# Delta rule's output projection as seven Strassen products over even and odd heads, with its weight sums made in DRAM and the gate sums moved into the attention

## The chip, the cores and the metric

The kernel runs on one core of one Trainium2 chip. The core has five engines that run side by side, each with an in-order queue of its own: PE (TensorE, matrix products), DVE (VectorE), ACT (ScalarE), POOL (GpSimd) and SP (SyncE, which mostly starts DMAs). They wait for each other by semaphores. The metric is the time of one execution on the device in microseconds (us), lower is better.

## The reference

One decoder layer on 512 tokens of 2048 channels, in float32. Two branches run from the same normalised input, and their gated sum goes through an output projection:

```python
mod = jax.nn.silu(c) @ w_ada + b_ada
shift, scale, gate = jnp.split(mod[:, None, :], 3, axis=-1)
h = rms_norm(x, norm_w) * (1.0 + scale) + shift
proj = h @ w_in
...
a_out = swa_attention(aq, ak, av, sinks).astype(x.dtype) * jax.nn.silu(ag)
y_a = a_out @ w_o_swa
...
o = gated_delta_rule(dq, dk, dv, g, beta)
o = rms_norm(o, dn_norm_w) * jax.nn.silu(dz.reshape(B, T, DN_V_HEADS, DN_HEAD_V).astype(f32))
y_b = o.reshape(B, T, DN_VAL).astype(x.dtype) @ w_o_dn

y = jax.nn.sigmoid(mg_a) * y_a + jax.nn.sigmoid(mg_b) * y_b
return x + gate * (y @ w_out)
```

The change concerns `o @ w_o_dn`, from 32 heads of 128 (4096 channels) to 2048, and where the sums for `gate` and the sums of the blocks of `w_out` are made.

## The kernel before

**Products.** Every large product is one stream of channel tiles on PE. `channel_tile` (line 244) takes 128 output channels for all 512 tokens: 16 steps over the contracted channels, and in each step `mm3` (line 237) issues three matmuls, high part by high part, high by low and low by high. The parts come from `split` (line 50): ACT casts a float32 tile to the type that PE takes (`hi`, line 52), DVE subtracts that from the tile (`lo`, line 53). The weights (128x128) are stationary, the tokens (512) move.

**Weights.** `plan` writes down the list of weight jobs in the order of use, 1 MB each for the projections. `load_job` (line 200) loads a job into one of two buffers `raw`; `split_half` splits half a job (128x1024) into one of three pairs `whi`, `wlo`; `half_done` marks the next split and, when both halves of a job are split, the next load.

**Order.** Behind every second step of a channel tile `pump()` is called, 8 times for a tile. It advances side jobs, which are generators: `go` starts one after so many pumps, `beside(gen, rate)` advances one at `rate` steps a pump. What the pump emits at that point stands there in the engines' queues. `drain` finishes such a job.

**Stages.** `startup`; `deltanet`, the heads in 16 pairs (scan, normalisation, gate z), with POOL working on the decay masks; `branch_b` (line 1023), which is rewritten; `attention` (line 1104); `finish`.

- In the heads' stage each pair ends with 8 transposes on PE (line 274, tile `pto`) and stores its two heads to `o_d`. Beside it `weight_sums`, at 0.13 steps a pump from the third pair on, copies x to the output and makes the sums of blocks of `w_out` in DRAM (tiles `wsm`): a copy of 1 MB from SP (line 684), and an accumulating DMA from POOL's queue (line 688) on top. `finish` has a Strassen step over `w_out` already and uses them.
- `branch_b` goes through the 4096 channels in two halves of 16 heads. For a half it loads `o_d` (16 pieces of 256 KB, `oraw`), splits it into `oh`, `ol`, computes two merge gates (channel tiles of another projection, into `ma_d`) and 16 channel tiles `od`. The first half's results go to `yb_d`; the second half's add them and multiply with (1 + `bth`), the other merge gate from `mb_d` (lines 1050 and 1051). Beside it, at 0.2, `gate` (line 1499) loads the 16 MB of its weights in pieces of 1 MB (`gw`, line 1505), multiplies each by one column of silu(c) and sums (DVE, line 1511), and closes with four matmuls by ones (`pgate`).
- `attention` computes keys, then four groups; a group is eight heads. `attend` (line 1230) works through four blocks of 128 tokens in a group, one chain each: scores `S` on PE (line 1249), mask and maximum on DVE (lines 1255, 1260), exponentials on ACT (line 1273, `sm`), the denominator `den` (line 1277) and the scaling of the eight heads on DVE (line 1281), transposes on PE (line 274, `pP`), products with the values (`O`, line 1300). In the queues the chains stand among the channel tiles of the group's projections.

## Time and profile before

| | |
|---|---|
| Time, median of 3 runs | 2922.81 us (2918.60 to 2924.77) |
| The profiled execution | 2922.19 us, of which the span is 2919.7 us |
| Granted TensorE clock, mean | 0.996 |
| PE busy | 98% of the span |
| DVE, ACT, POOL busy | 60%, 37%, 8% |
| Read from HBM, written | 429.42 MB, 97.20 MB |
| The heads' stage | up to about 1628 us |
| Output projection with its merge gates | 1628 to about 2030 us |
| Attention | 2057 to 2565 us |

The profile is one execution. A row of a group gives the line in the kernel, the engine, the operation and its tiles (output <- inputs), the shape, the count, then busy time, the mean length of one in ns, and how long the engine idled just before such instructions, with what ended most of it. A row of the timeline gives start, length, engine, line, tiles, and in brackets the idle time ahead of it and who ended it. A row of windows gives the stretch, its length, then the busy time of PE, PE's weight loads (PEld), DVE, ACT and POOL with the count of instructions, the granted clock, the share in which the DMA engines were busy, and GB/s.

### The profile page before, as it was taken

How to read it: one execution, taken by the hardware profiler on the slowest of the kernel's cores; microseconds unless marked ns; L12 is line 12 of the kernel's file. 1: busy time of each engine (PE TensorE's matmuls, PEld its weight loads, DVE VectorE, ACT ScalarE, POOL GpSimd, SP SyncE). 2: the span in 40 equal slices, each digit the busy share in tenths (PEclk: the TensorE clock that was granted, in tenths of full speed). 3: DMA queues.
4: the chain of work that ended last, by engine and by line, in shares of the span. 5: the costliest groups of instructions: out<-in, count | busy, mean ns of one | idle time of the engine just before them, and what ended most of it. 6: DMA issues, size and time to landing. Idle time of an engine off the chain costs nothing.

```text
span 2919.7 us, 37991 instructions
## 1 busy us (share of the span) xinstructions
PE 2868.2 (98%) x14556; PEld 2349.8 (80%) x14556; DVE 1740.0 (60%) x2853; ACT 1082.6 (37%) x2097; POOL 243.5 (8%) x234
## 2 busy tenths in 40 slices
PE   8899999999999999999999999999999999999999
PEld 6677888888888888888888788888788788788777
DVE  6775998777776554544444453434755655554565
ACT  4354333433334333333333322312334434432343
POOL 0022211101101111110000000000100000000010
PEclk9999999999999999999999999999999999999999
DMA  9747555635547664663332675554322223365575
GB/s 382 288 147 214 160 179 151 201 120 200 169 150 215 186 194 145 196 173 122 109 124 87 234 259 181 198 162 162 107 88 90 77 89 105 114 234 180 174 243 152
DMA packets 176615, 493.58 MB, mean 169 GB/s; under 512 B 72721, under 2 KB 75281, under 8 KB 134321
## 3 DMA queue, kind: packets, MB, share of 16 engines
q1 hardware_dynamic: 170834, 466.52, 47.3%
q0 software_dynamic: 5600, 24.64, 4.3%
q8 instruction: 114, 1.87, 0.3%
q14 instruction: 67, 0.55, 0.1%
HBM read 429.42 MB, written 97.20 MB: 180 GB/s over the span
## 4 chain that ended last, share of the span: by engine, by line
PE 87%; DVE 5%; issue 4%; ACT 2%; DMA 2%; POOL 1%; SPq 0%; DVEq 0%; POOLq 0%; ACTq 0%
PE mm L240 24%; PE mm L242 23%; PE mm L241 23%; PE m L241 1%; PE m L242 1%; PE m L240 1%; DVE wa L414 1%; PE S L1249 1%; PE pv L959 1%; PE po L978 1%; PE O L1300 1%; PE pP L274 1%; DVE wlo L53 1%; PE pd L974 1%; PE po L977 1%
## 5 line engine op out<-in xcount | busy, mean ns | idle before, releaser
L240 PE MATMUL mm<-hh,whi 128*128 128x512 f32 x2784 | 1132.0, 407 | 2.3 <-ACT whi L52 1.6
L242 PE MATMUL mm<-hh,wlo 128*128 128x512 f32 x2784 | 1090.6, 392 | 1.1 <-DVE wlo L53 1.1
L241 PE MATMUL mm<-hl,whi 128*128 128x512 f32 x2784 | 1088.1, 391 | 0.0
L53 DVE TENSOR_TENSOR wlo<-raw,whi 128x1024 fp32r<-128x1024 f32 (+1 forms) x428 | 527.3, 1235 | 497.5 <-ACT whi L52 492.8
L52 ACT CAST whi<-raw 128x1024 fp32r<-128x1024 f32 (+1 forms) x428 | 445.5, 1043 | 933.3 <-PE mm L241 905.5
L242 PEld LDWEIGHTS mm<-hh,wlo 128*128 128x128 f32 x2784 | 523.0, 188 | 115.3 <-DVE wlo L53 1.9
L240 PEld LDWEIGHTS mm<-hh,whi 128*128 128x128 f32 x2784 | 524.3, 188 | 112.7 <-issue 8.4
L241 PEld LDWEIGHTS mm<-hl,whi 128*128 128x128 f32 x2784 | 524.8, 189 | 99.2 <-issue 0.8
L240 PE MATMUL mm<-oh,whi 128*128 128x512 f32 x512 | 200.3, 393 | 1.1 <-ACT whi L52 0.9
L241 PE MATMUL mm<-ol,whi 128*128 128x512 f32 x512 | 199.4, 390 | 1.0 <-DVE ol L53 1.0
L242 PE MATMUL mm<-oh,wlo 128*128 128x512 f32 x512 | 199.4, 390 | 0.5 <-DVE wlo L53 0.5
L755 POOL TENSOR_TENSOR E<-E,neg_g 128x512 f32<-128x512 f32 x64 | 81.3, 1270 | 482.2 <-DMA E<-g_rows 331.3
L805 DVE TENSOR_TENSOR A<-A,atmp 128x62 f32<-128x62 f32 (+30 forms) x124 | 114.3, 922 | 1.5
L240 PEld LDWEIGHTS mm<-oh,whi 128*128 128x128 f32 x512 | 96.1, 188 | 22.8 <-ACT whi L52 1.3
L241 PEld LDWEIGHTS mm<-ol,whi 128*128 128x128 f32 x512 | 96.1, 188 | 22.6 <-DVE ol L53 2.0
L242 PEld LDWEIGHTS mm<-oh,wlo 128*128 128x128 f32 x512 | 96.1, 188 | 21.0 <-DVE wlo L53 1.3
L798 DVE TENSOR_TENSOR atmp<-A 128x62 f32<-128x62 f32 (+30 forms) x124 | 109.9, 886 | 1.5
L906 POOL TENSOR_TENSOR qe<-qe,yq 128x512 f32<-128x512 f32 x32 | 48.6, 1537 | 725.3 <-DMA qe<-eg_rows 617.6
L53 DVE TENSOR_TENSOR wlo<-raww,whi 128x1024 fp32r<-128x1024 f32 x56 | 68.2, 1221 | 41.3 <-ACT whi L52 41.3
L52 ACT CAST whi<-raww 128x1024 fp32r<-128x1024 f32 x56 | 59.0, 1053 | 75.5 <-PE m L242 66.3
L952 DVE SCALAR_TENSOR_TENSOR r<-pp,neg_eg,vt 128x128 f32<-128x128 f32 x96 | 29.2, 346 | 78.8 <-PE pp L949 77.6
L1273 ACT ACTIVATE sm<-sm,mx,rs 128x256 f32<-128x256 f32 (+1 forms) x128 | 71.7, 562 | 3.3 <-DVE mx L1268 3.3
(328 smaller groups left out, 3126.5 us busy)
## 6 DMA issues: line engine op xcount, KB each, us to landing
raw<-in_w_ch SPq DMA_DIRECT2D x158, 1024.0 KB
wa<-in_w_ada_ss SPq DMA_DIRECT2D x32, 1024.0 KB
raw<-in_w_od SPq DMA_DIRECT2D x32, 1024.0 KB
E<-g_rows SPq DMA_DIRECT2D x64, 256.0 KB
wsm<-in_w_out POOLq DMA_DIRECT2D x16, 1024.0 KB, 9.9
gw<-in_w_ada_gate SPq DMA_DIRECT2D x16, 1024.0 KB
raw<-in_w_os SPq DMA_DIRECT2D x16, 1024.0 KB
raww<-wsm SPq DMA_DIRECT2D x16, 1024.0 KB
```

Source lines behind the costliest of these rows:

```text
L52: self.nc.scalar.copy(out=hi, in_=src)
L53: self.nc.vector.tensor_tensor(out=lo, in0=src, in1=hi.bitcast(F32), op=ALU.subtract)
L240: nc.tensor.matmul(ps, lhsT=wh, rhs=xh, start=first, stop=False)
L241: nc.tensor.matmul(ps, lhsT=wh, rhs=xl, start=False, stop=False)
L242: self.last_mm = nc.tensor.matmul(ps, lhsT=wl, rhs=xh, start=False, stop=last).ins
L274: self.nc.tensor.transpose(dst[:, c * P : (c + 1) * P], src_cols(c), self.ident)
L755: nc.gpsimd.tensor_tensor(out=E, in0=E, in1=ng, op=ALU.add)
L798: eng.tensor_tensor(out=t, in0=A[:, m : m + 1, m + 1 :].to_broadcast([P, m, n]), in1=A[:, :m, m : m + 1].to_broadcast([P, m, n]), op=ALU.mult,
L805: eng.tensor_tensor(out=A[:, :m, m + 1 :], in0=A[:, :m, m + 1 :], in1=t, op=ALU.add)
L906: nc.gpsimd.tensor_tensor(out=qf, in0=qf, in1=q, op=ALU.mult)
L952: nc.vector.scalar_tensor_tensor(out=r[:, e, :], in0=pp[:, e, :], scalar=self.neg_eg[:, c, 2 * g + e : 2 * g + e + 1], in1=v[e][:, c, :], ...
L1273: nc.scalar.activation(t, t, AF.Exp, scale=r[:, h : h + 1], bias=mx[:, h : h + 1], accum_out=den[:, h : h + 1])
```

## The change

The 4096 x 2048 product is written as a 2x2 block product: the contracted channels are split into even and odd heads, the tokens into the first and last 256, the output channels into two blocks of 1024. It is computed with seven products of sums (a form of Strassen's) instead of eight.

- `head_sums`: when a pair of heads is done, its four operand sums are made (four DVE operations of 128x256, in the tile `osb`), and seven operands are stored to `oq_d` with three DMAs, in place of two for `o_d`.
- `od_sums`: four sums of weight blocks, 8 tiles of 1 MB each, are made in DRAM (`od_d`) beside the heads from the third pair on, at 0.08 steps a pump: 32 copies from SP and 32 accumulating DMAs from POOL. `weight_sums`, for `w_out`, moves to the attention at 0.17, with its copies of x.
- `branch_b`: seven products of 16 steps. In a step the activations (128 channels by 128 tokens) are stationary and the weights (512 of 1024 columns) move, for two blocks of columns and two of tokens, three matmuls each, and one pump. The operands come in pieces of 256 KB, split six ahead. Weight jobs: 56 of 1 MB in place of 32. Results are tokens by channels; `evict` combines them in `k1`, `k5` and `c` (ACT copies for m1 and m5, DVE for the rest), and `od_store` turns them with eight transposes on PE, multiplies with (1 + merge gate) and stores to `yb_d`. Two merge gates run before the products and two behind them. The PSUM pools become six buffers for results and two for transposes.
- `gate` moves to the attention at 0.48, in four passes of 512 columns: 64 loads of 256 KB into one buffer and 64 multiplications of 128x512, with the closing matmul at the end of each pass.

```diff
@@ plan
-        for half in range(2):
-            ma(range(5 + 2 * half, 7 + 2 * half))
-            jobs += [(f"od{half}_{j}", a["w_od"][half, j]) for j in range(KT)]
+        ma(range(5, 7))
+        for m, (name, _, w) in enumerate(self.od_order()):
+            src = a["w_od"][w] if w else self.od_d[name]
+            jobs += [(f"od{m}_{b}", src[b]) for b in range(8)]
+        ma(range(7, 9))
@@ deltanet
-                        self.beside(self.ordered(self.weight_sums()), 0.13, "ws")
+                        self.beside(self.ordered(self.od_sums()), 0.08, "ws")
...
+    def od_order(self):
+        return [
+            ("m1", 0, (0, 0)), ("m2", 1, (1, 0)), ("m5", 3, None), ("m6", 4, None), ("m7", 5, None), ("m4", 2, None),
+            ("m3", 6, (1, 1)),
+        ]
+
+    def od_sums(self):
...
+        steps = [
+            [("m7", w[0, 1]), ("m5", w[0, 0])], [("m7", w[1, 1]), ("m5", w[0, 1])],
+            [("m6", d["m7"])], [("m6", w[0, 0])], [("m4", d["m6"])], [("m4", w[1, 0])],
+        ]
+        for slot in range(20):
+            todo = [(n, src, b) for b in range(8) if 0 <= slot - 2 * b < 6 for n, src in steps[slot - 2 * b]]
+            for i, (n, src, b) in enumerate(todo):
+                if slot % 2:
+                    nc.gpsimd.dma_start(out=d[n][b], in_=src[b], accum_op=ALU.add, max_dma_last_dim=8192)
+                else:
+                    nc.sync.dma_start(out=d[n][b], in_=src[b], max_dma_last_dim=8192)
+                if i % 2:
+                    yield
+            if len(todo) < 3:
+                yield
...
+    def head_sums(self, g, z, s):
...
+        TT(out=s[:, 0], in0=z[0][:, hi], in1=z[1][:, hi], op=ALU.subtract)
+        STT(out=s[:, 1], in0=s[:, 0], scalar=-1.0, in1=z[0][:, lo], op0=ALU.mult, op1=ALU.subtract)
+        TT(out=s[:, 2], in0=z[0][:, lo], in1=z[0][:, hi], op=ALU.add)
+        STT(out=s[:, 3], in0=s[:, 1], scalar=-1.0, in1=z[1][:, lo], op0=ALU.mult, op1=ALU.subtract)
+        for q, src in ((slice(0, 1), z[0][:, lo].unsqueeze(1)), (slice(1, 3), z[1].rearrange("p (q t) -> p q t", q=2)), (slice(3, 7), s)):
+            nc.sync.dma_start(out=self.oq_d[q, g // 2].rearrange("q p k t -> p q k t")[:, :, g % 2, :], in_=src)
@@ branch_b
+            for m, (name, _, _) in enumerate(order):
+                ps = {}
                 for kt in range(KT):
...
+                    u = 8 * m + kt // 2
+                    if kt % 2 == 0:
+                        split(u + 6)
+                    oh, ol = parts[u]
+                    hi, lo = self.half(f"od{m}_{kt // 2}")
+                    for n in range(2):
+                        w = slice(n * T, n * T + T)
+                        for t in range(2):
+                            if kt == 0:
+                                ps[n, t] = self.pmm.tile([P, T], F32, tag="mm", name="od")
+                            x = (oh[:, kt % 2, t * P : t * P + P], ol[:, kt % 2, t * P : t * P + P])
+                            self.mm3(ps[n, t], x, (hi[:, w], lo[:, w]), kt == 0, kt == KT - 1)
+                            if kt == KT - 1:
+                                evict(name, n, t, ps[n, t])
+                        self.pump()
+                    self.half_done()
...
+    def od_store(self, wk, half, j, c):
...
+        for q in range(2):
+            pt = self.ptp.tile([P, 2, 256], F32, tag="tp", name="pty")
+            for i in range(2):
+                for t in range(2):
+                    s = slice((2 * q + i) * P, (2 * q + i) * P + P)
+                    nc.tensor.transpose(pt[:, i, t * P : t * P + P], c[t][:, s], self.ident)
+            yield 1
+            y = wk.tile([P, 2, 256], F32, tag="yb", name="yb", bufs=3)
+            nc.vector.scalar_tensor_tensor(out=y, in0=mb[q], scalar=1.0, in1=pt, op0=ALU.add, op1=ALU.mult)
+            yield 1
...
@@ attention
+            self.beside(self.ordered(self.weight_sums()), 0.17, "ws")
+            self.beside(self.gate(keep), 0.48, "gate")
@@ gate
-        for kt in range(KT):
-            w = wk.tile([P, D], F32, tag="gw", name="gw", bufs=1)
-            nc.sync.dma_start(out=w, in_=a["w_ada_gate"][kt])
...
+            acc = wk.tile([P, T], F32, tag="vch0", name="gate_bc")
+            for kt in range(KT):
+                w = wk.tile([P, T], F32, tag="vch1", name="gw")
+                nc.sync.dma_start(out=w, in_=a["w_ada_gate"][kt][:, sl])
+                yield
...
+                    nc.vector.scalar_tensor_tensor(out=acc, in0=w, scalar=s, in1=acc, op0=ALU.mult, op1=ALU.add)
+                yield
```

Two places show how the queues are moved. DVE in the attention, first chain of the third group, from the sum that finishes the maxima to the denominator (`wlo` is a weight split, `ao` the end of the chain before). Before:

```order
L1263 TENSOR_TENSOR mx<-mx,rs 128x8
L1264 TENSOR_TENSOR mx<-mx,sink 128x8
L1266 TENSOR_TENSOR es<-sink,mx 128x8
L1268 TENSOR_SCALAR mx<-mx 128x8
L53 TENSOR_TENSOR wlo<-raw,whi 128x1024
L1307 TENSOR_TENSOR ao<-O,sg 128x4x128
L1277 TENSOR_TENSOR den<-den,es 128x8
```

After:

```order
L1372 TENSOR_TENSOR mx<-mx,rs 128x8
L1373 TENSOR_TENSOR mx<-mx,sink 128x8
L1375 TENSOR_TENSOR es<-sink,mx 128x8
L1377 TENSOR_SCALAR mx<-mx 128x8
L1624 SCALAR_TENSOR_TENSOR gate_bc<-gw,silu_c,gate_bc 128x512
L53 TENSOR_TENSOR wlo<-raw,whi 128x1024
L1416 TENSOR_TENSOR ao<-O,sg 128x4x128
L1624 SCALAR_TENSOR_TENSOR gate_bc<-gw,silu_c,gate_bc 128x512
L1386 TENSOR_TENSOR den<-den,es 128x8
```

Two steps of the gate stand between the negated maximum and the denominator, where there were none. The second place is DVE at the end of the fifth product (m7) of the new stage, which has no counterpart before (`od` is a result in PSUM, `k` and `c` the tiles that it is combined into, `ol` the split of an operand):

```order
L53 TENSOR_TENSOR ol<-oraw,oh 128x512
L53 TENSOR_TENSOR wlo<-raw,whi 128x1024
L1097 TENSOR_TENSOR k_13984<-od,k_13984 128x512
L1098 TENSOR_TENSOR c<-od,k_13985 128x512
L1097 TENSOR_TENSOR k_13984<-od,k_13984 128x512
L1098 TENSOR_TENSOR c<-od,k_13985 128x512
L1097 TENSOR_TENSOR k_13984<-od,k_13984 128x512
L1098 TENSOR_TENSOR c<-od,k_13985 128x512
L1097 TENSOR_TENSOR k_13984<-od,k_13984 128x512
L1098 TENSOR_TENSOR c<-od,k_13985 128x512
L53 TENSOR_TENSOR wlo<-raw,whi 128x1024 x2
```

Eight evictions stand between one weight split and the next.

133 lines of the change are left out of this document (84 added, 49 removed).

## The prediction

> **What bounds the kernel now.** I read the engine totals first, then the chain of waits by engine, then the groups of instructions.
>
> ```profile
> PE 2868.2 (98%) x14556; PEld 2349.8 (80%) x14556; DVE 1740.0 (60%) x2853; ACT 1082.6 (37%) x2097; POOL 243.5 (8%) x234
> PE 87%; DVE 5%; issue 4%; ACT 2%; DMA 2%; POOL 1%; SPq 0%; DVEq 0%; POOLq 0%; ACTq 0%
> L240 PE MATMUL mm<-oh,whi 128*128 128x512 f32 x512 | 200.3, 393 | 1.1 <-ACT whi L52 0.9
> ```
>
> PE is busy for 98% of the span, and 87% of the chain that ended last lies on it. The third row is one of the three product kinds of the stage that the change rewrites: 512 matmuls, waiting 1.1 us in all. Whatever shortens PE's stream there shortens the kernel, as long as no other engine stops the stream. Windows cut at the stages (us; busy of PE, PEld, DVE, ACT, POOL; granted clock; DMA share; GB/s) show how much room there is:
>
> ```profile
> 600.00:700.00 100.00, 99.10 (x531) 82.34 (x530) 74.09 (x120) 38.42 (x88) 15.72 (x12) 1.00 0.47 156
> 700.00:800.00 100.00, 99.06 (x520) 82.05 (x519) 74.63 (x115) 36.18 (x79) 9.71 (x9) 1.00 0.59 178
> 1400.00:1500.00 100.00, 100.00 (x523) 83.56 (x523) 49.98 (x100) 36.95 (x90) 12.10 (x11) 1.00 0.39 122
> 1628.00:1660.00 32.00, 30.89 (x137) 24.69 (x137) 18.41 (x21) 12.19 (x17) 0.00 (x0) 1.00 0.79 268
> 1660.00:2030.00 370.00, 368.57 (x1616) 302.61 (x1615) 152.50 (x140) 92.12 (x107) 1.00 (x2) 1.00 0.59 201
> 2057.00:2565.00 508.00, 508.00 (x2856) 408.12 (x2856) 300.50 (x595) 205.11 (x445) 25.56 (x18) 1.00 0.29 97
> 2785.00:2850.00 65.00, 64.19 (x284) 52.71 (x283) 44.01 (x50) 28.27 (x30) 6.93 (x8) 1.00 0.82 247
> ```
>
> The heads run to about 1628, the output projection of the delta rule to 2030, the attention from 2057 to 2565. In every one PE idles by less than 1% or so, and the attention, which receives two moved side jobs, has no PE idle at all. So the gain is a count of matmuls, and the question is what the moved work does to the others.
>
> **The matmuls.** The change issues 1344 products for 1536: 192 fewer, of the same shape (128 stationary columns, 512 moving), whichever operand is stationary. Their spacing is read from two rows of the old stage, 75 matmuls apart (25 of each of the three kinds):
>
> ```profile
> 2009.64 0.39 PE L240 MATMUL mm<-oh,whi 128*128 128x512 f32 x1
> 2026.64 0.39 PE L240 MATMUL mm<-oh,whi 128*128 128x512 f32 x1
> ```
>
> 17.00 / 75 = 226.7 ns each (0.39 is one matmul's length, which overlaps the next). 192 x 226.7 ns = **-43.5 us**.
>
> **The transposes.** Results come out as tokens by channels, and 64 transposes of 128x128 turn them. The heads' own transposes give the price:
>
> ```profile
> 1627.84 1.26 PE L274 MATMUL pto<-ident,osb 128*128 128x128 f32 x8 [0.17 <-DVE osb L1009]
> 1628.85 0.49 PE L242 MATMUL mm<-hh,wlo 128*128 128x512 f32 x1
> ```
>
> Eight take PE from 1627.84 to 1628.85, 1.01 us, 0.126 us each: 64 are **+8.1 us**. Here the Trainium skill speaks against the change: its page "TensorE: Matmul & The Clock Gate", section "Part 4: PE-mode transpose", puts one transpose in a kernel's context at some 275 ns. By that figure the 64 would be an estimated 17.6 us and the time 2916; this case's rows disagree with it, at 0.126 for eight in a row, so it gets no chance of its own.
>
> **Waits that go.** The old stage begins by loading 16 pieces of o beside the 1 MB gate weights; the first of its two windows idles 1.1 us, the second 1.4. The new one prefetches four operands behind two merge gates and has no gate weights beside it: **-2.5 us** (bounds 0 and -2.5).
>
> **Sums of heads.** Four DVE operations of 128x256 for each of 16 pairs, by these rows of the finishing stage:
>
> ```profile
> L1370 DVE TENSOR_TENSOR ya<-ya,yc 128x256 f32<-128x256 f32 x6 | 2.5, 422 | 11.5 <-DMA yc<-y_d 11.5
> L1371 DVE SCALAR_TENSOR_TENSOR ya<-ya 128x256 f32<-128x256 f32 x6 | 2.5, 419 | 0.1
> ```
>
> 64 x 0.42 = 27 us of DVE over a stage in which DVE is busy 50 to 75 us of each 100 and PE 99 to 100: **0** (with the cover gone, 27). Three DMAs for a pair in place of two go on SP behind the same generator; nothing of that stage reads them.
>
> **Weight sums in the heads' stage.** There were 16 copies on SP and 16 accumulating DMAs on POOL from the third pair on; now there are 32 and 32, at 0.08 steps a pump for 0.13. PE's idle in the two windows from 600 to 800, where the first old ones fall, is 0.90 + 0.94 us; later windows have none. Twice that would be +1.8 and none at all is possible: I take **+1** (0 to +4, the upper end twice the doubled value, since POOL waits in order for each copy).
>
> **Evictions in the new stage.** 28 results, eight DVE operations together behind each of products four and five (m6, m7), and per store four multiplies.
>
> ```profile
> L1051 DVE SCALAR_TENSOR_TENSOR yb<-bth,yb x16: 691/692/693, 1861.4 to 2028.2; 128x512 f32<-128x512 f32 x16
> L53 DVE TENSOR_TENSOR wlo<-raww,whi 128x1024 fp32r<-128x1024 f32 x56 | 68.2, 1221 | 41.3 <-ACT whi L52 41.3
> ```
>
> Eight at 0.69 hold DVE 5.5 us, and one weight split (1.22) is queued behind them. A half of weights now lasts 12 matmuls, 2.72 us; three halves are kept, so PE has about 5.4 us of split weights when the block begins, against 5.5 + 1.2. That is a shortage of 1.3 us at two products, and less at the others, whose store multiplies (0.69 each) fall among splits. I take **+5** (0 to 12, twice the whole block and a multiply).
>
> **Raw weights.** A 1 MB load used to serve 48 matmuls, 10.9 us; it now serves 24, 5.44 us, with the same two buffers. A buffer's round is 10.88 us, of which the split of its two halves takes about 2.7 + 0.8, so a load has some 7.4 us. The gate weights of the same size, issued and used here, bracket it:
>
> ```profile
> 1723.66 0.33 SPq L1505 DMA_DIRECT2D gw<-in_w_ada_gate  x1
> 1730.97 2.35 DVE L1511 SCALAR_TENSOR_TENSOR gate_bc<-gw,silu_c,gate_bc 128x2048 f32<-128x2048 f32 x1 [4.16 <-DMA gw<-in_w_ada_gate]
> 1740.99 0.33 SPq L1505 DMA_DIRECT2D gw<-in_w_ada_gate  x1
> 1745.85 2.35 DVE L1511 SCALAR_TENSOR_TENSOR gate_bc<-gw,silu_c,gate_bc 128x2048 f32<-128x2048 f32 x1 [2.62 <-DMA gw<-in_w_ada_gate]
> ```
>
> 4.86 us alone, 7.31 with a load of raw weights beside it. The new stage moves 1 MB and a 256 KB operand each 5.44 us, 241 GB/s, less than the 247 and 268 of two windows above. Just below the threshold: **0** (bounds 0 and, at 8.5 us a load, 28 rounds x 1.1 = 31).
>
> **Gate sums and out's weight sums in the attention.** The four matmuls that finish the gate only move: 0. What costs is DVE's queue. Sixteen chains (scores, mask, maximum, exponentials on ACT, denominator, eight scalings, then transposes on PE) run one behind another, and PE reaches the transposes shortly after DVE has finished. The first chain of the first group, then the second, third and fourth of a group and the first of the next:
>
> ```profile
> 2123.21 0.17 DVE L1277 TENSOR_TENSOR den<-den,es 128x8 f32<-128x8 f32 x1 [4.00 <-ACT sm L1273]
> 2123.65 1.66 DVE L1281 TENSOR_SCALAR sm<-sm,den 128x128 f32<-128x128 f32 x8
> 2127.41 1.03 PE L274 MATMUL pP<-ident,sm 128*128 128x128 f32 x8
> ...
> 2277.69 0.17 DVE L1277 TENSOR_TENSOR den<-den,es 128x8 f32<-128x8 f32 x1 [4.86 <-ACT sm L1273]
> 2278.13 2.19 DVE L1281 TENSOR_SCALAR sm<-sm,den 128x256 f32<-128x256 f32 x8
> 2281.82 1.04 PE L274 MATMUL pP<-ident,sm 128*128 128x128 f32 x8
> ...
> 2305.29 0.17 DVE L1277 TENSOR_TENSOR den<-den,es 128x8 f32<-128x8 f32 x1 [4.86 <-ACT sm L1273]
> 2305.73 2.19 DVE L1281 TENSOR_SCALAR sm<-sm,den 128x256 f32<-128x256 f32 x8
> 2308.49 1.03 PE L274 MATMUL pP<-ident,sm 128*128 128x128 f32 x8
> ...
> 2333.19 0.17 DVE L1277 TENSOR_TENSOR den<-den,es 128x8 f32<-128x8 f32 x1 [1.70 <-ACT sm L1273]
> 2333.63 2.19 DVE L1281 TENSOR_SCALAR sm<-sm,den 128x256 f32<-128x256 f32 x8
> 2338.32 1.03 PE L274 MATMUL pP<-ident,sm 128*128 128x128 f32 x8
> ...
> 2350.59 0.17 DVE L1277 TENSOR_TENSOR den<-den,es 128x8 f32<-128x8 f32 x1 [2.11 <-ACT sm L1273]
> 2351.46 0.30 PE L274 MATMUL pP<-ident,sm 128*128 128x128 f32 x1
> ```
>
> From the end of the scalings to PE's transposes there are 2.10, 1.50, 0.57, 2.50 and no us (in the last the transposes follow the scalings one by one). In brackets is what DVE waits for ACT before the denominator: 4.00, 4.86, 4.86, 1.70, 2.11. By the order of DVE after the change, gate steps stand before the negated maximum in chains one to four of the groups 3, 2, 1, 2; 0, 0, 2, 2; 0, 0, 2, 1; 0, 1, 0, 0 times, and in the wait for ACT 2, 1, 0, 1; 1, 0, 1, 1; 2, 0, 1, 1; 2, 0, 0, 0 times. A step is 0.69 us and the wait w for its weights, whose single buffer is refilled only behind the step before; queued behind a step that waits are the chain's own operations and the weight splits that PE needs. The plan issues a load 1 / 0.48 = 2.08 pumps of six matmuls, 2.83 us, ahead of its use. Loads of this size:
>
> ```profile
> 1655.03 2.65 DMA oraw<-o_d
> 746.89 5.69 DMA qe<-eg_rows
> ```
>
> 2.65 with little beside it, 5.69 beside the copies of x to the output, which now move here too: w lies between 0 and 2.86. A chain is late by its steps before the maximum, plus what its other steps exceed ACT's wait by, less the margin. Summed over the sixteen: w = 0 gives 1.7 us, 1.0 gives 16, 2.0 gives 40, 2.86 gives 63. The 36 moved copies of 1 MB, at 4.86 to 7.31 us each, run for 175 to 263 of 508 us, so w averages 1.0 to 1.5; the attention's DMA share is only 0.29, half that of the window of the slow load, so I take 1.0: **+16 us** (2 to 63). The Trainium skill, "DMA: Bandwidth & Descriptors", section "Issuing engines are not separate DMA queues", says that transfers started by any engine share the 16 DMA engines and interleave. The two rows agree as far as they go; it gives no price, and by it moving the sums to POOL's queue would not spare the gate's loads.
>
> **The sum.** -43.5 + 8.1 - 2.5 + 0 + 1 + 5 + 0 + 16 = -15.9, against the profiled execution: its span is 2919.7 us, with 2.5 around it 2922.19, 0.6 below the median 2922.81. 2922.19 - 15.9 = 2906.3: **2906 us**.
>
> **Rivals.** *All hidden* (0.13): evictions fit between splits and gate loads arrive in time, -43.5 + 8.1 - 2.5 + 2 = -36, 2886 us. For it: the idle PE of 0 in the attention and DVE at 300 of 508. Against it: the margin of 0.57 us, less than one step.
>
> *Two raw buffers starve the products* (0.13): loads at 8.0 us cost 28 x 0.6 = 17, at 8.5 us 31, so 2923 to 2937. For it: 7.31 measured beside one other load. Against: the old stage's pair of streams was fetching 1 MB in 7.6 us and 1 MB in 10.9 us at once, some 236 GB/s, and PE lost little.
>
> *The attention is held by the single gate buffer* (0.19), slower than before: every load comes late, w from 2.0 to 2.86, 40 to 63 us, so 2930 to 2953. It decides from the point where it eats the 31.9 gained elsewhere, w = 1.65, a load of 4.5 us. For it: 5.69, and DVE queues the next chain behind a step that waits. Against: DMA share 0.29.
>
> That the products aren't fewer can't be: the change's order on PE has the 1344 and the 64 transposes.
>
> **How the numbers follow.** The forecast has 0.55, with its own range 2892 (w = 0) to 2919. The range 2887 to 2930 adds most of the first rival, half of the second and the low end of the third. This kernel's measurement tells 0.2%, 5.8 us, from no change. Faster by more: 0.53 of the forecast, 0.13, and 0.05 of the starved case, 0.71; within: 0.02 + 0.03 + 0.02 = 0.07; slower: 0.05 + 0.17 = 0.22.
>
> **What would show it.** In the profile after: the products' stage from the first product's matmul to the last should take 1344 x 0.2267 = 305 us, with transposes, the two merge gates before and evictions near 340; PE idle in it under 6 us, and with none ending on a load of raw weights. The matmul's spacing stays at 227 ns, the transposes cost about 8 us. The windows up to 1628 stay within 4 us. The attention grows by about 16 us, in stalls of 1 to 3 us before transposes, released by DVE's scaled scores, with DVE waiting for gate weights before them. Wrong it would be if a stall appears on raw weights again and again, if PE waits over 30 us in the attention, or if the heads' stage loses more than a few us to POOL's waits.

## The result, and the profile after

The change makes the kernel slower: 2964.7 us median of 4 runs (2959.45 to 2967.60) against 2921.15 us of the kernel before on the same chips, a ratio of 1.0146 with a 95% interval of 1.0125 to 1.0167. The profiled execution, the shortest of the four, took 2959.45 us with a span of 2957.7, 38.0 more than the 2919.7 before; the account below is of that one.

The engine totals and the chain of waits by engine of the kernel after the change:

```profile
PE 2851.2 (96%) x14428; PEld 2333.2 (79%) x14428; DVE 1854.2 (63%) x3052; ACT 1140.6 (39%) x2161; POOL 270.9 (9%) x266
PE 51%; DMA 7%; DVE 5%; issue 2%; ACT 1%; SPq 0%; POOL 0%; DVEq 0%; POOLq 0%; ACTq 0%
```

PE is busy for 17 us less, not 35, and its idle time went from 51.5 to 106.5 us; DMA stands in the chain with 7% where it had 2%. To see where, the span is cut at three marks on PE: the last transpose of the heads (`pto`), the first transpose of v (`ptva`, in the attention's first tile) and the last product with the values (`O`). The tile views give them, before (first two rows; 1628.8 for `pto` stands in the table) and after:

```profile
L1154 PE MATMUL ptva<-ident,vch x8: 270/272/273, 2035.5 to 2039.0; 128*128 128x128 f32 x8
L1300 PE MATMUL O<-pT,vtok_a x448: 272/273/324, 2131.1 to 2567.4; 128*64 128x128 f32 x150
```

```profile
L276 PE MATMUL pto<-ident,osb x128: 270/272/328, 615.6 to 1660.1; 128*128 128x128 f32 x128
L1263 PE MATMUL ptva<-ident,vch x8: 270/272/276, 2023.9 to 2027.4; 128*128 128x128 f32 x8
L1409 PE MATMUL O<-pT,vtok_a x448: 272/273/324, 2131.7 to 2606.2; 128*64 128x128 f32 x150
```

| stretch | before | after | difference | predicted |
|---|---|---|---|---|
| start to last `pto` (heads) | 1628.8 | 1660.1 | +31.3 | +1 |
| to first `ptva` (the seven products) | 406.7 | 363.8 | -42.9 | -33 |
| to last `O` (attention) | 531.9 | 582.3 | +50.4 | +16 |
| to the end | 352.3 | 351.5 | -0.8 | 0 |
| span | 2919.7 | 2957.7 | +38.0 | -16 |

The products brought more than forecast; the side jobs that came with them cost nearly twice that in two other stages. Windows of the changed kernel (same columns as before) show the shape of the loss, and the one stage that runs clean:

```profile
800.00:900.00 100.00, 88.88 (x458) 73.97 (x457) 65.97 (x121) 32.89 (x81) 9.10 (x10) 0.95 0.68 199
1200.00:1300.00 100.00, 90.07 (x461) 74.92 (x460) 42.14 (x81) 33.37 (x76) 11.04 (x12) 0.95 0.80 231
1700.00:1800.00 100.00, 100.00 (x451) 82.81 (x450) 61.36 (x63) 49.23 (x58) 0.00 (x0) 1.00 0.74 259
2023.90:2606.20 582.30, 550.17 (x2975) 436.31 (x2975) 356.72 (x684) 214.08 (x457) 40.05 (x34) 0.96 0.60 182
```

In the attention PE idles 582.3 - 550.2 = 32.1 us, and the granted clock is 0.96, so what it does takes longer too: 550.2 us of busy time for work that takes 533.0 in a run without the stalls (b2 below). In the heads two stalls, of 11.1 and 9.9 us, carry most of it. In the waits of PE over the heads there is one row that counts:

```profile
PE pd L1001 <- DVE vs L993: 26.1, 4, 11.1
```

PE waits for DVE's `vs` 4 times, 11.1 us in the longest. The timeline around that one, SP first, then POOL, ACT, DVE and PE:

```profile
829.27 0.64 SPq L687 DMA_DIRECT2D od_m<-in_w_od  x1
832.79 0.53 SPq L687 DMA_DIRECT2D od_m<-in_w_od  x1
833.41 0.59 SPq L202 DMA_DIRECT2D raw<-in_w_ch  x1
827.29 1.68 POOL L685 DMA_DIRECT2D od_m<-in_w_od  x2
846.97 0.81 POOL L685 DMA_DIRECT2D od_m<-in_w_od  x1 [18.00 <-DMA od_m<-in_w_od]
851.57 0.82 POOL L685 DMA_DIRECT2D od_m<-in_w_od  x1 [3.80 <-DMA od_m<-in_w_od]
857.87 1.04 ACT L52 CAST whi<-raw 128x1024 fp32r<-128x1024 f32 x1 [13.57 <-DMA raw<-in_w_ch]
858.95 1.23 DVE L53 TENSOR_TENSOR wlo<-raw,whi 128x1024 fp32r<-128x1024 f32 x1 [14.67 <-ACT whi L52]
862.11 1.22 PE L1001 MATMUL pd<-vs,k 128*128 128x256 f32 x2 [11.12 <-DVE vs L993]
```

A load of raw weights is issued at 833.41 and is there at 857.87, after 24 us, with four accumulations from POOL and two copies around it. DVE waits at the split of these weights, the scan's `vs` stands behind that split in its queue, and PE waits for `vs`. So PE doesn't wait for weights, but for a bystander of theirs. In the attention the same happens by way of the gate's weights:

```profile
2202.51 11.86 SPq L1618 DMA_DIRECT2D gw<-in_w_ada_gate  x2
2201.88 1.68 POOL L715 DMA_DIRECT2D wsm<-in_w_out  x2
2213.27 0.75 DVE L1624 SCALAR_TENSOR_TENSOR gate_bc<-gw,silu_c,gate_bc 128x512 f32<-128x512 f32 x1 [8.78 <-DMA gw<-in_w_ada_gate]
2220.03 2.07 PE L1358 MATMUL S<-kd,aq 64*128 64x256 f32 x6 [6.74 <-DVE sm L1364]
```

Two accumulations start at 2201.88, the gate's load right behind them at 2202.51 (the row merges it with the next one); the step that uses it runs at 2213.27, and PE's next scores wait 6.74 us for the masks that stand behind that step and behind a second one, which waits another 2.87. DVE's waits over the whole stage (us, times, longest):

```profile
DVE gate_bc L1624 <- DMA gw<-in_w_ada_gate: 98.0, 35, 13.2
DVE gate_bc L1622 <- DMA gw<-in_w_ada_gate: 11.4, 3, 5.7
DVE aq L1207 <- POOL aq L1204: 1.2, 1, 1.2
```

109.4 us of them are for gate weights; POOL itself, whose rotation multiplies stand behind its accumulations, kept DVE waiting for 1.2. Nor is it POOL in the heads: PE and DVE wait for nothing of POOL's there from 600 us on, and ACT waits 81.1 us for its masks where it waited 77.7 before.

### The profile page after: what moved, and what is told of

It is laid out like the page before. It is cut to its first block, busy times and chain, and to the rows that moved or that the text cites. A ratio compares the mean times of both kernels' runs of the same rounds, so it can differ in the third digit from the quotient of the medians.

```text
span 2957.7 us, 38403 instructions
## 1 busy us (share of the span) xinstructions
PE 2851.2 (96%) x14428; PEld 2333.2 (79%) x14428; DVE 1854.2 (63%) x3052; ACT 1140.6 (39%) x2161; POOL 270.9 (9%) x266
## 3 DMA queue, kind: packets, MB, share of 16 engines
q1 hardware_dynamic: 199688, 529.45, 53.2%
HBM read 523.79 MB, written 166.40 MB: 233 GB/s over the span
## 4 chain that ended last, share of the span: by engine, by line
PE 51%; DMA 7%; DVE 5%; issue 2%; ACT 1%; SPq 0%; POOL 0%; DVEq 0%; POOLq 0%; ACTq 0%
PE mm L242 10%; PE mm L244 10%; PE mm L243 10%; DMA gw<-in_w_ada_gate 5%; PE od L244 3%; PE od L243 3%; PE od L242 3%; DMA raw<-in_w_ch 2%; PE m L243 1%; PE m L244 1%; PE m L242 1%; ACT sm L1382 1%; DVE wlo L53 1%; DVE gate_bc L1624 1%; PE po L1005 1%
## 5 line engine op out<-in xcount | busy, mean ns | idle before, releaser
L53 DVE TENSOR_TENSOR wlo<-raw,whi 128x1024 fp32r<-128x1024 f32 (+1 forms) x476 | 583.6, 1228 | 431.4 <-ACT whi L52 428.3
L52 ACT CAST whi<-raw 128x1024 fp32r<-128x1024 f32 (+1 forms) x476 | 495.1, 1043 | 827.6 <-PE mm L243 665.6
L242 PE MATMUL od<-whi,oh 128*128 128x512 f32 x448 | 174.8, 391 | 0.0
L243 PE MATMUL od<-wlo,oh 128*128 128x512 f32 x448 | 174.4, 389 | 0.0
L244 PE MATMUL od<-whi,ol 128*128 128x512 f32 x448 | 174.4, 389 | 0.0
L1624 DVE SCALAR_TENSOR_TENSOR gate_bc<-gw,silu_c,gate_bc 128x512 f32<-128x512 f32 x60 | 46.9, 782 | 98.0 <-DMA gw<-in_w_ada_gate 98.0
L244 PEld LDWEIGHTS od<-whi,ol 128*128 128x128 f32 x448 | 84.1, 188 | 17.3
L243 PEld LDWEIGHTS od<-wlo,oh 128*128 128x128 f32 x448 | 84.2, 188 | 17.2
L242 PEld LDWEIGHTS od<-whi,oh 128*128 128x128 f32 x448 | 84.1, 188 | 17.2
```

The costliest lines, as they stand in the source:

```text
L52: self.nc.scalar.copy(out=hi, in_=src)
L53: self.nc.vector.tensor_tensor(out=lo, in0=src, in1=hi.bitcast(F32), op=ALU.subtract)
L242: nc.tensor.matmul(ps, lhsT=wh, rhs=xh, start=first, stop=False)
L243: nc.tensor.matmul(ps, lhsT=wh, rhs=xl, start=False, stop=False)
L244: self.last_mm = nc.tensor.matmul(ps, lhsT=wl, rhs=xh, start=False, stop=last).ins
L1624: nc.vector.scalar_tensor_tensor(out=acc, in0=w, scalar=s, in1=acc, op0=ALU.mult, op1=ALU.add)
```

## The experiments

All start from the changed kernel, and the first three marks above are what is compared. "Attention" is the stretch from the first `ptva` to the last `O`. Where no interval stands, the run has one time, beside 2919 to 2922 us of the kernel before. How far a mark moves by itself shows in the runs that have a stage alike: without od sums the last `pto` lay at 1630.6 and 1631.0, with the sums as after the change at 1660 to 1672 (seven runs), with one DMA a step at 1634 to 1639 (six runs); the attention with gate and sums as after took 578 to 582 us (four runs).

### The heads: what makes the raw weights late

**h1**, without the od sums:

```diff
-    self.beside(self.ordered(self.od_sums()), 0.08, "ws")
-            src = a["w_od"][w] if w else self.od_d[name]
+            src = a["w_od"][w or (0, 0)]
```

> Leaves the sums of od weight blocks out (the products read blocks of w_od itself); the head sums and their stores stay. Measure: the start of the last transpose of the heads' stage (pto), 1628.8 us before the change and 1660.1 after it. Theory 'sums' DMAs' (raw weights wait behind the copies and accumulations): it falls back to 1629 +/- 4, and the whole to about 2932. Rival 'head sums' (the four DVE operations and the three stores of a pair hold the scan): it stays at 1655 to 1660.

2928.95 us, last `pto` 1630.6. The sums' DMAs cost the heads; the head sums and their stores don't.

**h2**, the same DMAs one a step:

```diff
-                if i % 2:
-                    yield
-            if len(todo) < 3:
-                yield
+                yield
+            for _ in range(4 - len(todo)):
+                yield
...
-self.od_sums()), 0.08
+self.od_sums()), 0.16
```

> The same sums, the same number of DMAs over the same stretch, but one DMA a step at twice the rate in place of two a step. Theory 'bursts' (raw weights are late because several copies and accumulations stand before them at once): the last pto falls by 15 to 31 us, to between 1629 and 1645. Rival 'bytes' (it is the amount moved, 96 MB read and written more): it stays above 1650. Attention and products as after the change.

2935.25 us, last `pto` 1638.5: some 70% of the loss goes with the same bytes. The bunching counts for more than the amount. From 600 us to the last `pto`, ACT waits 18.5 us for raw weights, for 33.6 after the change.

**e2** came last, after the attention's runs had put the accumulations under suspicion: they become plain copies from SP.

```diff
-    nc.gpsimd.dma_start(out=d[n][b], in_=src[b], accum_op=ALU.add, max_dma_last_dim=8192)
+    nc.sync.dma_start(out=d[n][b], in_=src[b], max_dma_last_dim=8192)
```

> The changed kernel with the 32 accumulating DMAs of the od sums replaced by plain 1 MB copies from SP at the same steps (the sums are left out, their bytes fall by a third of the accumulations'). Last pto 1660 to 1672 in runs with the accumulations, 1638 with one DMA a step, 1631 without any. Theory 'accumulations from POOL's queue make SP's loads late', as d2 and d3 show for the attention: 1631 to 1642. Rival 'bursts on SP's own queue' (raw weights stand behind copies): above 1655.

2936.01 us. The tile view:

```profile
L276 PE MATMUL pto<-ident,osb x128: 270/272/329, 616.6 to 1635.2; 128*128 128x128 f32 x128
```

1635.2, still two a step, with as many transfers and more of them on SP, and ACT's waits for raw weights are 3.0 us. The rival, raw weights behind copies in SP's own queue, falls: what makes them late is the accumulations. Whether that is because POOL starts them or because each occupies the DMA engines longer (the prices are below), this run can't tell.

### The attention: gate, weight sums, or both

**a1**, one of 16 gate steps in each pass, and **a2**, one load for the 16 steps of a pass:

```diff
# a1
-            for kt in range(KT):
+            for kt in range(1):
# a2
-                w = wk.tile([P, T], F32, tag="vch1", name="gw")
-                nc.sync.dma_start(out=w, in_=a["w_ada_gate"][kt][:, sl])
+                if kt == 0:
+                    w = wk.tile([P, T], F32, tag="vch1", name="gw")
+                    nc.sync.dma_start(out=w, in_=a["w_ada_gate"][kt][:, sl])
```

> Leaves 15 of 16 steps of the gate's sums out, in each of the four passes, loads and multiplications; out's weight sums stay in the attention. Measure: from the end of the products (start of the first key tile, 2027 before the change, 2015 after it) to the last product with the values (O), 540 us before, 591 after. Theory 'gate' (the steps and the waits for their weights in DVE's queue): 540 to 550. Rival 'weight sums' (the copies delay raw weights and the partners of the rotation): above 570.

> Loads only the first piece of gate weights of each pass and multiplies it 16 times: 60 loads of 256 KB left out, the 64 DVE steps stay. Theory 'late loads': as without the gate, plus 2 to 8 us, so 542 to 558 us from products to the last O. Rival 'DVE time' (64 x 0.75 us in a queue that PE waits for): 570 to 591.

a1: 2925.72 us, attention 538.8 (547 by the mark of its expectation, whose first tile starts some 8 us ahead of `ptva`): the sums alone cost 7 us. a2: 2934.56 us, attention 552.1 (560 by that mark, 2 over the upper end). The 60 loads are worth 30 us; the 60 DVE steps 13 beside the sums, more than the 1.7 that the prediction gave them at w = 0.

**b2**, the gate alone, without out's weight sums:

```diff
-                    for dst, src, _ in parts:
-                        nc.sync.dma_start(out=dst, in_=src, max_dma_last_dim=8192)
...
-                    for dst, _, more in parts:
-                        nc.gpsimd.dma_start(out=dst, in_=more, accum_op=ALU.add, max_dma_last_dim=8192)
```

> Leaves the sums of out's weight blocks out of the attention (its four copies of x stay); the gate stays with its single buffer. From the transposes of v (ptva) to the last O: 532 before the change, 582 after, 539 without the gate. Theory 'planned too late' (a gate load is issued 2.83 us ahead and takes longer even with nothing beside it): 565 to 575. Rival 'copies slow the gate loads': 540 to 555.

2917.97 us, and the attention takes 535.0 us, nearly its old 531.9:

```profile
2028.10:2563.10 535.00, 532.99 (x2977) 426.00 (x2975) 355.81 (x684) 213.08 (x456) 26.28 (x18) 1.00 0.41 135
```

```profile
DMA gw<-in_w_ada_gate: 47.1, 33
```

Below the range of either theory. DVE still waits 47.1 us for gate weights, in 33 waits of at most 3.7, and they fall into its slack: PE idles 2.0 us. The gate alone costs 3, the sums alone 7, both together 50. Neither is at fault by itself, and the single buffer isn't either.

**b1**, the changed kernel without od sums, gate steps and out's sums (the edits of h1, a1 and b2 together):

> All three side jobs left out at once: no sums of od weights, 15 of 16 gate steps left out, no sums of out's weights (the products read plain blocks). What stays of the change is the seven products, their transposes, the head sums. If the losses of the heads (31) and of the attention (51) come from the side jobs alone and don't overlap, the span is 2919.7 - 43.6 + 2 = 2878 +/- 4. If the head sums, the new operand stores or the reordering themselves cost, it stays above 2885.

2883.12 us, span 2880.8. The seven products are worth what the count of matmuls says (38.9 us; -43.5 + 8.1 - 2.5 is -37.9), and the losses come from the side jobs alone. The attention takes 534.0 us here, 2 more than before, with the gate's closing matmuls still in it. From this base the gate's steps alone cost 1, the sums alone 5, both 48.

**c1**, out's sums and the copies of x in pieces of 256 KB, four times as many steps (of the edit, the lines that cut the copies of the sums):

```diff
-                    for dst, src, _ in parts:
-                        nc.sync.dma_start(out=dst, in_=src, max_dma_last_dim=8192)
+                    for q in range(4):
+                        r = slice(32 * q, 32 * q + 32)
+                        for dst, src, _ in parts:
+                            nc.sync.dma_start(out=dst[r], in_=src[r], max_dma_last_dim=8192)
+                            yield
...
-self.weight_sums()), 0.17
+self.weight_sums()), 0.7
```

> Computes everything. The changed kernel with one thing altered: out's weight sums in the attention go in pieces of 256 KB, four times as many steps. Same bytes, same gate with its single buffer. From the transposes of v (ptva) to the last O: 582 with pieces of 1 MB, 535 without these sums, 539 without the gate. Theory 'size of the piece' (a gate load waits for a whole 1 MB copy or accumulation ahead of it, 6 to 10 us): 540 to 555. Rival 'bytes' (the DMA engines are shared, so any order of the same bytes makes loads as late): 570 to 585.

2952.56 us, attention 567.1, between the two theories. DVE's waits for gate weights halve to 52.4 us, about b2's, but PE loses 20.6 us in waits of at most 4.8 us at other places, 6.0 of them for the rotated queries. What delays these was not followed up.

**d2**, the copies of out's sums from POOL as well, and **d3**, the accumulations as plain copies from SP:

```diff
# d2
-                        nc.sync.dma_start(out=dst, in_=src, max_dma_last_dim=8192)
+                        nc.gpsimd.dma_start(out=dst, in_=src, max_dma_last_dim=8192)
# d3
-                        nc.gpsimd.dma_start(out=dst, in_=more, accum_op=ALU.add, max_dma_last_dim=8192)
+                        nc.sync.dma_start(out=dst, in_=more, max_dma_last_dim=8192)
```

> Computes everything. The changed kernel, with the 16 copies of out's weight sums started from POOL's queue in place of SP's; bytes, pieces of 1 MB and the gate as after the change. ptva to last O: 582 after the change. Theory 'own queue' (a gate load waits because the copy stands before it in the DMA queue that SP feeds): gate waits on DVE halve from 109 us, 540 to 560. Rival 'shared engines' (whatever queue a copy comes from, it takes the same DMA engines): waits 90 to 115, 570 to 590.

> The accumulating DMAs of out's weight sums replaced by plain copies of the same 1 MB from SP (the sums are left out, their bytes fall by a third of the accumulations' traffic). ptva to last O: 582 after the change. Theory 'POOL's queue' (the rotation's multiplies stand behind accumulations that wait for copies): 545 to 560, with POOL's waits for copies gone. Rival 'DMA ahead of the gate loads': 565 to 585, gate waits on DVE still 80 to 115 us.

d2: 3015.82 us, the worst of all; d3: 2926.46 us. The windows of their attention, d2 first:

```profile
2035.80:2661.90 626.10, 559.67 (x2977) 443.92 (x2975) 359.33 (x684) 214.08 (x457) 49.54 (x50) 0.94 0.57 169
```

```profile
2032.30:2572.40 540.10, 537.50 (x2975) 428.13 (x2975) 356.60 (x684) 213.09 (x456) 27.32 (x18) 0.99 0.58 196
```

DVE's largest row of waits for gate weights, d2 and d3:

```profile
DVE gate_bc L1624 <- DMA gw<-in_w_ada_gate: 115.8, 38, 7.3
```

```profile
DVE gate_bc L1624 <- DMA gw<-in_w_ada_gate: 63.7, 33, 6.7
```

d3 has more transfers in the queue in which the gate's loads stand, the same DMA share (0.58 for 0.60), more GB/s (196 for 182), and loses only 8 us to the kernel before. Its loads are not all in time, DVE waits 65.9 us for them with a second row, but the longest wait is 6.7 for 13.2 and PE idles 2.6 us. So most of the attention's 50 us goes with the accumulations beside the gate. The theory of POOL's in-order queue forecast 545 to 560 for d3, whose accumulations no longer wait there, and 540.1 lies 5 us under that; against it stands the row of the changed kernel in which DVE waits 1.2 us for POOL.

d2 moves the same bytes as the changed kernel and takes the copies out of the gate's queue; it should have helped if that queue were the trouble, and costs 44 us more. It lies beyond both its theories, with 127.2 us of waits for gate weights. It looks as if it mattered which engine starts a transfer, but the edit does a second thing: in POOL's queue the copies stand behind the rotation's multiplies, which wait for their operands, and then come in a row with the accumulations. The last eight transfers of the sums start within 45 us (2498.30 to 2543.15), in the changed kernel within 95 (2460.04 to 2555.04). No run tells starter from bunching here. The queue tables add a price, after the change first, then d3, then d2:

```profile
q1 hardware_dynamic: 199688, 529.45, 53.2%
q0 software_dynamic: 10208, 58.20, 9.9%
```

```profile
q1 hardware_dynamic: 201992, 546.22, 55.5%
q0 software_dynamic: 7904, 41.42, 7.0%
```

```profile
q1 hardware_dynamic: 197384, 512.67, 50.8%
q0 software_dynamic: 12512, 74.98, 11.4%
```

(Packets, MB, share of the 16 DMA engines over the span.) 16 accumulations less are 2.9% less, 9.9% of 2957.7 against 7.0% of 2924.4: 88 us, 5.5 each. The plain copies in their place add 55.5% of 2924.4 less 53.2% of 2957.7 to SP's queue: 49.5 us, 3.1 each. In d2 16 plain copies add 51 us to POOL's queue, 3.2 each, and take 42 from SP's, 2.6 each. So a plain copy occupies the engines for 2.6 to 3.2 us, about the same whoever starts it, and an accumulation nearly twice as long. (The shares are rounded to 0.1%, which leaves about 0.2 us each way.) By the profile's count of HBM traffic nothing fell: 523.79 MB read and 166.40 written in all three runs. Since d3 and e2 change the starter, the price and, without POOL's queue, the moment of the start together, they don't tell which of them makes the loads late. The Trainium skill has a rule that would fit the starter, on "DMA: Bandwidth & Descriptors", section "SWDGE vs HWDGE vs iDMA": in each DMA engine the transfers of GpSimd and those of SP feed different queues, between which the engine takes turns. If so, one transfer from POOL might get as many turns as all that SP has queued. No run here shows the turns themselves.

### Versions that compute everything

**b3** and **c2** keep the gate in the attention and issue its next load right behind the step that frees the buffer; b3 spreads the od sums as h2, c2 cuts both sums into pieces of 256 KB, one a step. (h2, c1 and d2 compute everything too.)

```diff
-                w = wk.tile([P, T], F32, tag="vch1", name="gw")
-                nc.sync.dma_start(out=w, in_=a["w_ada_gate"][kt][:, sl])
                 yield
...
                     nc.vector.scalar_tensor_tensor(out=acc, in0=w, scalar=s, in1=acc, op0=ALU.mult, op1=ALU.add)
-                yield
+                if kt < KT - 1:
+                    w = load(c * KT + kt + 1)
```

> Computes everything. The od sums one DMA a step (as in h2), and the gate's next load issued right behind the step that frees its buffer, one step every four pumps, so 5.4 us ahead instead of 2.83. Theory 'late loads': ptva to last O falls from 582 to 552 to 560 and the whole to 2905 to 2915. Rival 'any DVE step in the chain costs' : 570 or more, whole above 2922.

> Computes everything. Both sums (od's beside the heads, out's in the attention) in pieces of 256 KB, and the gate's loads issued right behind the step that frees the buffer. Theory 'size of the piece': last pto at 1630 to 1640 (1660 before the cut), ptva to last O 535 to 550, the whole 2890 to 2905. Rival 'bytes': last pto above 1650, attention above 570, the whole above 2930.

b3: 2937.19 us, 1.0059 (1.0042 to 1.0076), attention 580.9, DVE waits for gate weights 98.6 us, 11.2 in the longest. Twice the lead gains next to nothing. The numbers are those of its rival, that any DVE step in the chain costs, but b2 has the same steps and loses 3. c2: 2936.66 us, 1.0047 (1.0030 to 1.0063), last `pto` 1651.8, attention 566.5, by two of three marks its rival's. In the heads pieces of 256 KB are worse than whole tiles one a step (1634 to 1639), though ACT waits for no raw weights there; what else they delay was not followed up.

**b4**, **c3** and **f1** put the gate beside the seven products; b4 and f1 spread the od sums as h2, c3 cuts both sums into 256 KB. f1 has four gate buffers for b4's two.

```diff
# branch_b
+            self.beside(self.gate(wk), 0.3, "gate")
# attention
-            self.beside(self.gate(keep), 0.48, "gate")
# gate, f1
+                w = wk.tile([P, T], F32, tag="gw", name="gw", bufs=4)
```

> Computes everything. The od sums one DMA a step; the gate moved out of the attention to the seven products (0.3 a pump, two buffers of 256 KB), where DVE has no chain that PE waits for but the weight splits. If the products have room in DVE (62 of 100 us) and DMA (0.7): the products stay at 355 us, the attention at about 540, the whole 2890 to 2900. If the raw weights starve beside 16 MB more (then 290 GB/s): the products grow by 15 or more and it is no better than 2905.

> Computes everything. As b4 (gate beside the seven products with two buffers), and both sums in pieces of 256 KB. Theory 'size of the piece': heads 2 to 8 us shorter than b4's 1638, attention at 535 to 540, the whole 2900 to 2906. If pieces are not what matters: as b4, 2912 +/- 3.

> Computes everything. As b4 (gate beside the seven products, od sums one DMA a step, out's sums alone in the attention) with four buffers of gate weights in place of two, loads three to four steps ahead, 0.27 a pump, and the closing matmuls behind a pause. In b4 DVE waited 38.9 us for gate weights, 27 times, ahead of weight splits, and the products took 322 us from first to last for 310 without the gate. If those waits are what they lost: products 312 to 316, the whole 2900 to 2908, 0.5 to 0.7% under the kernel before. If it is DMA (raw weights were waited for too, 53 us on ACT): products stay at 318 to 326 and the whole at 2908 to 2916.

b4: 2912.01 us, 0.9976 (0.9963 to 0.9988), products 321.8 us from first to last, attention 540.4: the products grow by 12 us, and the whole stays above the range for room in that stage. c3: 2939.02 us, 1.0060 (1.0045 to 1.0075), a miss: pieces of 256 KB make the last `pto` 1646.4 and the attention 555.4 instead of helping. f1: 2907.57 us, **0.9965 (0.9952 to 0.9978)**, the fastest that computes everything, but not for the reason given: its products took 322.4 us,

```profile
L242 PE MATMUL od<-whi,oh x448: 387/389/798, 1655.8 to 1978.2; 128*128 128x512 f32 x150
```

as long as b4's. DVE still waits 38.4 us for gate weights, 38.9 in b4, and raw weights are late there (ACT waits 63 us for them, 35 times): it is DMA, at 297 GB/s in that stretch, and more buffers don't help. f1's profiled execution beats b4's by 6 us outside the products, 4 in the heads and 2 in the rest, of which none was aimed at; the heads' 4 are within the 1634 to 1639 above, and the two intervals overlap, so f1 isn't shown to be faster than b4.

**d1** and **e1** put the gate into the last stage, beside the attention's projection; e1 sets the closing matmuls of the passes back by six to ten pumps.

```diff
# finish
+                self.ptp = eo.enter_context(tc.tile_pool(name="ptpf", bufs=2, space=PSUM, reuse_waits="tile"))
+                self.beside(self.gate(wk), 0.62, "gate")
# gate, e1
+            self.go(self.gate_close(wk, sl, acc), 6)
```

> Computes everything. The od sums one DMA a step (as h2), out's weight sums alone in the attention, and the gate in the last stage, beside the 16 channel tiles of the attention's projection (0.62 a pump, two buffers of 256 KB). If the gate and out's weight sums only hurt each other side by side, the products stay at 310 us from first to last (b4: 322), ptva to last O at about 540, and from the last O to the end 351 plus what the gate costs there: 0 to 10. The whole 2897 to 2908. If that stage has no room either (its PE idled 5.5 us of 100 already), above 2912.

> Computes everything. As d1, with the closing matmul of each pass six to ten pumps (8 to 14 us) behind its last step in place of one or two: in d1 PE waited 20.4 us in four of them for DVE. From the last O to the end 386 us in d1; if those waits are all, 362 to 368 here and the whole 2893 to 2900, faster than the kernel before by 0.7 to 1.0%. If DVE simply hasn't the room in that stage, the waits move to the weight splits and the whole stays above 2908.

d1: 2916.38 us, 0.9982 (0.9972 to 0.9992). Its attention takes 530.4 us, but from the last `O` to the end 386. PE's waits there:

```profile
PE pgate L1635 <- DVE gate_bc L1628: 20.4, 4, 7.3
```

e1: 2916.91 us, 0.9988 (0.9979 to 0.9997), 381 us to the end, and 13.2 us of the same wait. So the closing matmuls for the most part only showed that DVE runs late there: it waits 51 us for gate weights in that stage, ahead of its other work. That expectation failed by its own rival.

## Why the prediction was wrong

**Right.** The matmuls: the products ran at the old spacing, 1344 x 0.2267 = 304.7 us, and from the first to the last took 310:

```profile
L242 PE MATMUL od<-whi,oh x448: 389/389/486, 1681.8 to 1991.4; 128*128 128x512 f32 x150
L244 PE MATMUL od<-whi,ol x448: 389/389/401, 1682.2 to 1991.9; 128*128 128x512 f32 x150
```

The remaining 5.6 us hold the 48 transposes that fall in between, 0.117 each for the 0.126 of the sum. The 275 ns that the Trainium skill gives for a transpose in a kernel's context ("TensorE: Matmul & The Clock Gate", "Part 4: PE-mode transpose") are the length of one record here too, 270 to 276, but successive ones overlap, so that figure is a length and not a price. Two raw buffers were enough, as taken; the rival that they starve the products falls. The head sums cost nothing that h1 could show. The evictions were put at +5 and cost nothing: every weight split came in time. The 2.5 us of waits went too: PE idles for none of that stretch after. Of the -42.9 in the table about 4 us are no gain: the gate's closing matmuls, 4.1 us of PE before the change,

```profile
L1519 PE MATMUL pgate<-gate_bc,ones x8: 590/592/594, 1863.3 to 1886.8; 128*128 128x512 f32 x8
```

now stand in the attention, and add 2 to 4 to its +50.4.

**Wrong, the heads.** The step was "PE's idle in the two windows from 600 to 800 ... Twice that would be +1.8", and a range to +4. It scaled the cost by the number of transfers. The old sums put at most two transfers at one step and left two steps behind them; the new ones run three tiles staggered, so that four copies or four accumulations come in two steps, and the next kind right behind. One load of raw weights then came after 24 us. Spreading gave back 22 of the 31, and plain copies 25, which the scatter of that mark doesn't tell apart. The way to PE was not the one that the range allowed for, POOL's waits: it was DVE's queue, in which the scan stands behind a weight split.

**Wrong, the attention.** "A chain is late by its steps before the maximum, plus ..." was the right path, gate loads to DVE's queue to PE, and the third rival had it at 40 to 63 us; measured were 50. The term that was mis-sized is w, "so I take 1.0". Its upper bound came from a load beside copies of x, which SP starts. No row was sought for a load beside an accumulation, though the change sets 16 of them next to the gate. Over all 64 steps w was 109.4 / 64 = 1.7, with single waits to 13.2, where 2.86 was the bound. For 1.7 the prediction's own sums give some 33 us, and PE idles 32.1; but an average is not what sets the cost: b2's w is 47.1 / 64 = 0.7, for which those sums give some 12, and it cost 1 to 3; its longest wait is 3.7. So the rival's number came out partly by luck, at a w below its 2.0 and with a term that it didn't have. Its point was wrong as well: it blamed the single buffer. b2 has that buffer and loses 3 us; b3 loads twice as early and gains next to nothing.

**Left out.** Behind a long stall PE also had a lower clock. After the wait of 6.74 us shown above, matmuls take 0.63 us until 2227.16 and then 0.39 again:

```profile
2224.61 0.63 PE L242 MATMUL mm<-hh,whi 128*128 128x512 f32 x1
2228.03 0.39 PE L242 MATMUL mm<-hh,whi 128*128 128x512 f32 x1
```

The granted clock is 0.50 from 2220 to 2224, 0.56 to 2228 and 1.00 from there to 2235. Over the attention PE was busy for 550.2 us, 17 more than in b2, at a granted clock of 0.96 for 1.00: a third of the loss there is not waiting. The row 800 to 900 of the heads has 0.95, behind the wait of 11 us, but over the heads from 600 us on PE's busy time grew by only 2 us, so there the loss is waiting. The sum had no term for a lower clock.

## What to carry to other kernels

Work that is moved off a busy engine must be priced with what it will stand next to: here each of two side jobs was nearly free in the attention and the two together cost 50 us. Before moving DMAs, find in the trace a load beside a transfer of the very kind that will be moved, accumulations from POOL apart from copies from SP, and see which instruction of which in-order queue uses it, and who stands behind it. Price its longest wait, not the average. Where side transfers had to overlap loads that PE soon needs, here in the heads, one at a time gave back 22 of 31 us with the same bytes, and whole pieces one at a time did better than pieces of 256 KB.

## What the runs showed of the hardware

A 1 MB accumulating DMA from POOL occupied the DMA engines for 5.5 us, a plain copy of 1 MB 2.6 to 3.1 from SP and 3.2 from POOL. Loads from SP beside accumulations from POOL came 24 us after their issue (1 MB) and 11 us (256 KB) in the two stalls shown, where the rows of the prediction have 4.9 to 7.3 and 2.7 to 5.7; the DMA share and GB/s of the attention hardly differed from a run in which DVE waited 66 us for them in place of 109 and PE for 2.6 in place of 32 (0.60 and 182 against 0.58 and 196). So a stage's DMA share didn't tell whether its loads were late. Behind a wait of 6.74 us PE ran at half the granted clock for some 7 us. The Trainium skill's sentence that DMAs interleave on the same engines regardless of the engine that started them ("DMA: Bandwidth & Descriptors", "Issuing engines are not separate DMA queues") agrees with the price of a plain copy, 2.6 to 3.1 and 3.2; whether the starter changes how long others wait, no run here tells apart from bunching and from the price of an accumulation.
